# Moving the first fills of the output projection to a later scan step, and spacing them closer

## The chip, the cores and the metric

The kernel runs on one core of a Trainium2 chip. The metric is the device time of one execution in microseconds, lower is better. The times of the kernel before are 2384.92 us (median of three runs, 2384.02 to 2391.09).

## What is computed

The reference is one layer of a latent generator, with 2048 latent tokens, 256 context tokens and a width of 1024. Cut to its skeleton:

```python
h = modulate(rms_norm(x))                                # and the same of the context
u = h @ w_in                                             # columns: pool, SSD, gated DeltaNet
lat = concat([pool_branch(u), ssd(u), gdn(u)]) @ w_out   # widths 256, 384, 384
x = x + m2 * lat
h2 = modulate(rms_norm(x))
x = x + m5 * expert_choice_ffn(h2)                       # 16 experts, each takes 256 tokens
return rms_norm(x) * g
```

SSD and gated DeltaNet ("GDN") are recurrent scans in both directions. The output projection multiplies 1024 mixed columns by `w_out`. Of these the first 256 (the pool branch) are ready before the scans begin, the next 384 come from SSD, the last 384 from GDN.

## The kernel before

The work runs in five phases. Phase A projects the inputs and convolves, phase B runs the scans, phase C does the rest of the output projection and the router, phase D chooses each expert's tokens, and phase E runs the experts. Products of 32-bit numbers are made of three matmuls on split operands (`mm3`, lines 132 to 135), so every such matmul shows up on L133, L134 and L135.

The change lies in phase B. Its body is one loop over `n` (from line 1270), which issues in each pass:

- `gdn_prep(n)` (L997): the small products of GDN's step `n`, written to `xk` and `XQ`, for 36 steps;
- the SSD tiles that `ssd_seq[n]` lists: first `ssd_b` (the backward states), then from pass 9 on `ssd_f`, whose part `ssd_out` (L877 to L934) makes one of 16 output tiles and stores it to the scratch tensor `mix_d`;
- seven pieces of the triangular inverses (`gdn_inv`, L1054), which come in 7 batches, each with 31 column steps on VectorE (L1071, L1073), then transposes (L1079 to L1082) and merges;
- from pass 9 on one step of the recurrent chain, `gdn_chain` (L1115): a subtraction on VectorE (L1135, `gR`), matmuls to PSUM tiles `pc` and `po`, the new state `gS` (L1163). The last 16 steps also make GDN's output (`gdn_out`, L1180), which goes to the scratch tensor `go_d` (L1192);
- and, by a running count, fills.

A fill (`fill_0`, `fill`, L1213 to L1236) is the part of the output projection that needs no scan: the pool branch's 256 rows for one tile of 128 tokens and one half of the 1024 columns. There are 32 fills. Each loads 128 KB of `mix_d` (`fm`, L1219) and 256 KB of the input (`fx`, L1221), splits `fm` on ScalarE and VectorE (`fmh`, `fml`), makes 6 matmuls of 128x512 into the PSUM tile `po` or, for every second one, `pm`, adds on VectorE (L1226) and stores 256 KB (L1227). `po` and `pm` have one buffer each and are shared: `po` with the chain's output, `pm` with the inverses' merges. The first fill of a half also loads the weights (`load_wout`, L1204 to L1210).

The count that places the fills is this:

```python
        rate += FR                    # L1307, FR = 0.7
        if rate >= GRP:               # GRP = 2
            rate -= GRP
            for f in todo[:GRP]:
                f()
            todo = todo[GRP:]
        rate = min(rate, GRP)
        n += 1
    for f in todo:                    # whatever is left when the loop ends
        f()
```

The loop has 45 passes (0 to 44): the chain's step `k` is issued in pass 9 + k. So pairs of fills are issued in passes 2, 5, 8, 11, 14, 17, 20, 22, 25, 28, 31, 34, 37, 40 and 42, and one pair after the loop.

The order of issue isn't the order on the engines. The program is built with a scheduler that reorders by priority: an instruction's place in the program is its priority, and `tc.high_priority` moves the chain, the first steps' products and the inverses ahead. Once built, each engine and each queue runs its instructions strictly as they stand. SP's queue issues nearly all DMAs of this phase, and an issue that waits for its data holds up the issues behind it.

Phase C follows: for each tile `prep(t)` loads `mix_d` (`mx`, L1378), `go_d` (`go`, L1380) and the sums so far (L1383), transposes `go` on TensorE (L1390), and `project(t)` multiplies by the remaining rows of `w_out`. Of these rows' weights, those of the second columns' half that belong to SSD (`wr`, `woh`, `wol`) are loaded to where SSD's tiles were.

## Time and profile before

| what | value |
|---|---|
| runs listed | 2391.09, 2384.92, 2384.02 us |
| median | 2384.92 us |
| span of the profiled execution | 2391.4 us |
| time of the profiled execution beside its span | not listed apart; the first run listed, 2391.09 us, is nearest to the span |
| TensorE, VectorE, ScalarE, GpSimd busy | 87%, 72%, 45%, 35% of the span |
| phase B, from the first SSD state to the last chain step | about 780 to 1452 us |
| phase C, TensorE at work on it | 1461 to about 1650 us |

The span is the stretch between the first and the last instruction of the profiled execution. Busy shares are averages over phases with different limits, so the profile is read phase by phase.

### The profile page before, as it was taken

What the parts mean: (1) busy time and instruction counts of PE and PEld (TensorE: products, weight loads), DVE (VectorE), ACT (ScalarE), POOL (GpSimd) and SP (SyncE); (2) the same over time, 40 slices, a digit from 0 to 9 for tenths busy, and PEclk for the clock granted to TensorE, in tenths of its full rate; (3) what the DMA queues carried; (4) which work ended last, traced back from release to release, by engine and by line L of the source; (5) the groups of instructions that cost most, each with busy time, mean ns of one, the idle gap of its engine ahead of it and who ended that gap; (6) DMA issues with size and microseconds to landing.
All of it is one profiled execution on the core that took longest, in us unless ns stands there. A gap on an engine that the chain in (4) does not pass through costs nothing. (4 is left out here: it accounts for less than half of the span.)

```text
span 2391.4 us, 44610 instructions
## 1 busy us (share of the span) xinstructions
PE 2084.4 (87%) x16769; PEld 1797.7 (75%) x16769; DVE 1733.0 (72%) x3635; ACT 1077.5 (45%) x2136; POOL 834.8 (35%) x755
## 2 busy tenths in 40 slices
PE   5789999999988667999988797996499999988886
PEld 2778888888867556778777676884489999978775
DVE  7666776877754698998898765546656766788876
ACT  5443333443314345556654442554144444455552
POOL 1002333355331435454453442445221111133453
PEclk8899999999989778999997898998699999998998
DMA  7433234433323997999876675655268778788883
GB/s 236 123 92 97 80 116 122 135 102 94 94 66 80 233 245 188 217 217 221 191 191 165 163 179 192 209 199 182 84 193 243 218 227 229 222 268 284 293 272 141
DMA packets 418033, 424.72 MB, mean 178 GB/s; under 512 B 151987, under 2 KB 312602, under 8 KB 416794
## 3 DMA queue, kind: packets, MB, share of 16 engines
q1 hardware_dynamic: 398106, 368.33, 53.6%
q0 software_dynamic: 14816, 50.03, 8.0%
q10 hardware_dynamic: 4896, 3.51, 0.5%
q8 instruction: 133, 2.18, 0.4%
q14 instruction: 82, 0.67, 0.1%
HBM read 309.55 MB, written 112.22 MB: 176 GB/s over the span
## 5 line engine op out<-in xcount | busy, mean ns | idle before, releaser
L1641 ACT ACTIVATE wh<-wr 128x1024 fp32r<-128x1024 f32 x192 | 202.1, 1056 | 255.5 <-PE pgate L134 74.7
L133 PE MATMUL pj<-hTh,wh 128*128 128x512 f32 (+1 forms) x800 | 308.1, 385 | 5.3 <-ACT wh L192 4.4
L461 DVE SCALAR_TENSOR_TENSOR acc<-u,PV,acc 128x512 f32<-128x512 f32 (+1 forms) x320 | 281.9, 930 | 39.1 <-ACT acc L459 21.1
L135 PE MATMUL pj<-hTh,wl 128*128 128x512 f32 (+1 forms) x800 | 306.9, 384 | 3.5 <-DVE wl L193 3.5
L134 PE MATMUL pj<-hTl,wh 128*128 128x512 f32 (+1 forms) x800 | 309.0, 386 | 0.0
L1643 DVE TENSOR_TENSOR wl<-wr,wh 128x1024 fp32r<-128x1024 f32 x176 | 221.3, 1263 | 104.8 <-ACT wh L1641 101.4
L133 PEld LDWEIGHTS pj<-hTh,wh 128*128 128x128 f32 x800 | 153.7, 192 | 37.4 <-ACT wh L192 4.7
L135 PEld LDWEIGHTS pj<-hTh,wl 128*128 128x128 f32 x800 | 153.3, 192 | 34.5 <-DVE wl L193 4.2
L134 PEld LDWEIGHTS pj<-hTl,wh 128*128 128x128 f32 x800 | 153.4, 192 | 29.6 <-issue 0.7
L506 POOL TENSOR_TENSOR aw<-aw,sc 128x1024 f32<-128x1024 f32 x32 | 68.4, 2139 | 251.1 <-DMA aw<-in_ada_w_dram 233.0
L134 PE MATMUL pgate<-xel,wh 128*128 128x256 f32 x512 | 151.0, 295 | 3.0 <-DVE xel L193 3.0
L133 PE MATMUL pgate<-xeh,wh 128*128 128x256 f32 x512 | 149.3, 292 | 3.6 <-ACT xeh L192 3.5
L135 PE MATMUL pgate<-xeh,wl 128*128 128x256 f32 x512 | 150.3, 294 | 0.0
L133 PE MATMUL pup<-xeh,wh 128*128 128x256 f32 x512 | 148.6, 290 | 0.0
L135 PE MATMUL pup<-xeh,wl 128*128 128x256 f32 x512 | 146.9, 287 | 0.0
L134 PE MATMUL pup<-xel,wh 128*128 128x256 f32 x512 | 146.7, 287 | 0.0
L1740 POOL DMA_INDIRECT x_d<-ye,idx x30 | 48.9, 1631 | 206.0 <-DVE ye L1734 128.6
L1071 DVE TENSOR_TENSOR tmpb<-Wb,Vb 128x31 f32<-128x31 f32 (+15 forms) x217 | 107.7, 496 | 5.7 <-POOL Vb L1063 1.9
L1073 DVE TENSOR_TENSOR Vb<-Vb,tmpb 128x31 f32<-128x31 f32 (+15 forms) x217 | 108.7, 501 | 3.7
L133 PE MATMUL pdown<-wh,hh 128*128 128x512 f32 x256 | 104.6, 408 | 7.6 <-DVE ye L1734 3.3
L133 PEld LDWEIGHTS pgate<-xeh,wh 128*128 128x128 f32 x512 | 101.4, 198 | 5.0 <-ACT xeh L192 4.6
L134 PEld LDWEIGHTS pgate<-xel,wh 128*128 128x128 f32 x512 | 101.6, 198 | 3.2 <-DVE xel L193 3.2
(581 smaller groups left out, 5927.8 us busy)
## 6 DMA issues: line engine op xcount, KB each, us to landing
wr<-in_exp_w_gate_dram SPq DMA_DIRECT2D x64, 512.0 KB
wr<-in_exp_w_up_dram SPq DMA_DIRECT2D x64, 512.0 KB
wr<-in_exp_w_down_dram SPq DMA_DIRECT2D x64, 512.0 KB
aw<-in_ada_w_dram SPq DMA_DIRECT2D x32, 512.0 KB
kv<-kv_d SPq DMA_DIRECT2D x72, 192.0 KB
xb<-xb_d SPq DMA_DIRECT2D x35, 320.0 KB
wr<-in_w_in_dram SPq DMA_DIRECT2D x21, 512.0 KB
aw<-in_ada_w_dram SPq DMA_DIRECT2D x8, 1024.0 KB
```

The source lines that it names most:

```text
L133: TE.matmul(o, lh, rh, start=start, stop=False, **kw)
L134: TE.matmul(o, lh, rl, start=False, stop=False, **kw)
L135: TE.matmul(o, ll, rh, start=False, stop=stop, **kw)
L461: V.scalar_tensor_tensor(av, u[:, s0 - 2 + i:s0 - 2 + i + w], cw[:, i, cb:cb + 1], av, op0=OP.mult, op1=OP.add)
L506: G.tensor_tensor(w, w, sc2[:, :, 0:1].to_broadcast([P, KT, P]), op=OP.mult)
L1071: V.tensor_tensor(t, W[:, c + 1:, c:c + 1].to_broadcast([P, nr, ncl]), N[:, c:c + 1, :ncl].to_broadcast([P, nr, ncl]), op=OP.mult)
L1073: V.tensor_tensor(N[:, c + 1:, :ncl], N[:, c + 1:, :ncl], t, op=OP.subtract)
L1641: S.activation(wh, w, AF.Copy)
L1643: (G if nw[0] <= 16 else V).tensor_tensor(wl, w, wh.bitcast(F32), op=OP.subtract)
L1740: G.indirect_dma_start(out=x2_d, out_offset=rows_of(e, h), in_=ys[h], in_offset=None, compute_op=OP.bypass if late else OP.add)
```

## The change

The running count starts at the ninth pass (`n` = 8), and it grows by 0.85 a pass instead of 0.7. Nothing else that reaches the engines is edited; the same diff also deletes comments and docstrings, and every line below the new constant stands one line lower.

```diff
@@ -51,7 +51,8 @@
 NPS = 3
 HPP = 2000
 LATE = 7
-FR = 0.7
+FR = 0.85
+NF0 = 8
 HPI = 500
 NHI = 2
 GRP = 2
@@ -1304,7 +1305,7 @@
         if n == NSTEP:
             load_1()
-        rate += FR
+        rate += FR if n >= NF0 else 0.0
         if rate >= GRP:
```

Pairs are now issued in passes 10, 12, 15, 17, 19, 22, 24, 26, 29, 31, 33, 36, 38, 40 and 43, and again one pair after the loop: as many as before, with three pairs fewer up to pass 8.

Since priorities follow the place in the program, the scheduler now lays out the whole of phase B in another order. Three places matter here.

The first is SP's queue at the start of phase B, from the first loads of SSD's tiles (`xb`) on. `kz`, `kq` and `kqg` are GDN's loads, `fx` and `fm` a fill's. Before:

```order
L843 DMA xb<-xb_d 128x640 x2
L775 DMA fsr_d<-rows 18x6x128 x4
L1204 DMA fx<-mrow_d 128x512
L1207 DMA fx<-in_w_out_dram 128x512 x2
L843 DMA xb<-xb_d 128x640
L1219 DMA fm<-mix_d 128x256
L1010 DMA kz_6202<-qk_d 64x6x64 x2
L1010 DMA kz_6203<-qk_d 64x6x64 x2
L1221 DMA fx<-in_x_dram 128x512
L1219 DMA fm<-mix_d 128x256
L1221 DMA fx<-in_x_dram 128x512
L1219 DMA fm<-mix_d 128x256
```

After:

```order
L844 DMA xb<-xb_d 128x640 x2
L776 DMA fsr_d<-rows 18x6x128 x4
L883 DMA cb<-bc_d 128x4x128
L887 DMA zt<-z_d 128x384
L964 DMA kqg<-qk_d 64x6x128
L844 DMA xb<-xb_d 128x640
L1011 DMA kz_6202<-qk_d 64x6x64 x2
L1011 DMA kz_6203<-qk_d 64x6x64 x2
L967 DMA kqg<-qk_d 64x6x64 x2
L1011 DMA kz_6202<-qk_d 64x6x64
L982 DMA eg<-gx_d 64x12x64
L1011 DMA kz_6202<-qk_d 64x6x64
```

Up to the fourth `kz` transfer the weights' loads and a `fm` load of the first fill are gone, and loads of `cb`, `zt` and `kqg` that stood further down stand here. The first fill's loads now stand some 70 rows further down.

The second place is TensorE's end of phase B. `gS` to `pc` is the chain's product of its last step (L1133 before, L1134 now), `po<-vn` the last product of a step, `ps<-fSR` the beginning of an SSD output tile and `ps<-ident,sy` its end. Before:

```order
L1169 MATMUL po<-vn_6220,XQr 64x64 x6
L1159 MATMUL pc<-vn_6220,ke 64x64 x12
L1169 MATMUL po<-vn_6220,XQr 64x64 x6
L1133 MATMUL pc<-gS_6224,kqg 64x64 x12
L1144 MATMUL po<-gS_6224,kqg 64x64 x12
L932 MATMUL ps<-ident,sy 128x128 x3
L1151 MATMUL pc<-gR,Yt_6206 64x64 x12
L1169 MATMUL po<-vn_6221,XQr 64x64 x12
```

After:

```order
L1145 MATMUL po<-gS_6224,kqg 64x64 x12
L1152 MATMUL pc<-gR,Yt_6206 64x64 x12
L136 MATMUL pm<-fh,fml 128x512
L134 MATMUL pm<-fh,fmh 128x512
L135 MATMUL pm<-fl,fmh 128x512
L136 MATMUL pm<-fh,fml 128x512
L933 MATMUL ps<-ident,sy 128x128 x3
L852 MATMUL ps<-xw,xb 128x192 x2
L892 MATMUL ps<-fSR 128x384
L893 LDWEIGHTS identb
L893 MATMUL ps<-sneg,identb 128x384
L1170 MATMUL po<-vn_6221,XQr 64x64 x12
```

Before, `ps<-ident,sy` is the end of the last SSD tile, and it stands ahead of the chain's last two products. Now it is the end of the last tile but one, and it stands behind the chain's last product but one (`pc<-gR,Yt`); the last tile only begins (`ps<-fSR`) ahead of the chain's very last product. The last tile's own end comes 20 rows further down; the eight small products of the router's bias and then phase C's first transposes follow directly behind it.

The third place is SP's queue at the same end. Before:

```order
L934 DMA mix_d<-syT 128x384
L1192 DMA go_d<-oe_14950 2x32x384 x2
L1378 DMA mx<-mix_d 128x768
L1204 DMA wr<-mrow_d 128x512
L1207 DMA wr<-in_w_out_dram 128x512 x3
L1227 DMA x_d<-fx 128x512
L1378 DMA mx<-mix_d 128x768
L1192 DMA go_d<-oe_15029 2x32x384 x2
L1380 DMA go<-go_d 128x384
```

After:

```order
L1193 DMA go_d<-oe_15029 2x32x384 x2
L1384 DMA xo<-x_d 128x512 x2
L1402 DMA mrow_15250<-mrow_d 128x1024
L1402 DMA mrow_15252<-mrow_d 128x1024
L1406 DMA g2row<-in_norm_g_dram 128x1024
L1410 DMA rw<-in_router_w_dram 128x8x16
L1412 DMA c_15259<-mcol_d 128x16
L1384 DMA xo<-x_d 128x512 x6
L935 DMA mix_d<-syT 128x384
L1379 DMA mx<-mix_d 128x768
L1381 DMA go<-go_d 128x384
L1205 DMA wr<-mrow_d 128x512
```

Before, the store of the last SSD tile (`mix_d<-syT`) stands first and the loads of `mx` and of the weights `wr` follow ahead of the last store of GDN's output (`go_d`). Now the last `go_d` store comes first, then loads that need no scan, then the last SSD tile's store, and only behind it `mx`, `go` and `wr`.

## Rows read from the trace of the kernel before

**Rows 1.** Busy time by stretch: stretch, length, engines' busy (instructions), clock, DMA share, GB/s

```profile
780.00:892.00 112.00, 73.37 (x597) 58.90 (x597) 86.84 (x174) 46.33 (x124) 47.48 (x62) 0.72 0.99 242
892.00:1340.00 448.00, 390.61 (x5607) 339.03 (x5606) 401.14 (x810) 253.90 (x751) 203.64 (x211) 0.92 0.82 197
1340.00:1450.00 110.00, 97.95 (x1338) 86.01 (x1339) 70.82 (x151) 48.92 (x146) 53.79 (x55) 0.92 0.63 162
1475.00:1640.00 165.00, 164.10 (x958) 135.43 (x957) 80.69 (x251) 80.96 (x204) 69.37 (x29) 0.99 0.59 205
```

**Rows 2.** DMAs of 780 to 892 us: total, then issues with KB of each

```profile
DMA packets 41665, 27.13 MB, mean 242 GB/s; under 512 B 26296, under 2 KB 36712, under 8 KB 41655
...
fx<-in_x_dram SPq DMA_DIRECT2D x8, 256.0 KB
...
x_d<-fx SPq DMA_DIRECT2D x6, 256.0 KB
...
fm<-mix_d SPq DMA_DIRECT2D x9, 128.0 KB
```

**Rows 3.** Groups of DVE instructions of 780 to 892 us: count | busy, mean ns | idle before

```profile
L193 DVE TENSOR_TENSOR fml<-fm,fmh 128x256 fp32r<-128x256 f32 x8 | 4.5, 565 | 4.4 <-ACT fmh L192 4.4
...
L1226 DVE TENSOR_TENSOR fx<-po,fx 128x512 f32<-128x512 f32 x4 | 2.7, 681 | 0.6 <-PE po L135 0.6
```

**Rows 4.** The same of 1340 to 1450 us, two operations of an SSD tile

```profile
L899 DVE TENSOR_TENSOR sE<-ps,sE 128x384 f32<-128x384 f32 x8 | 4.1, 549 | 0.1
L894 DVE TENSOR_TENSOR sE<-sE,sEb 128x768 f32<-128x768 f32 x4 | 3.8, 956 | 6.1 <-ACT sEb L893 6.1
```

**Rows 5.** DVE in order of time: start, us; first inverse, first chain subtraction

```profile
813.37 2.04 DVE L1065 STREAM_TRANSPOSE Wb<-Db 64x1024 f32<-64x1024 f32 x1 [1.36 <-ACT Db L1043]
...
891.79 0.54 DVE L1135 TENSOR_TENSOR gR<-kv,pc 128x384 f32<-128x384 f32 x1
```

**Rows 6.** Who waited for whom, 892 to 1460 us: total us, times, longest

```profile
PE po L1144 <- DVE fx L1226: 12.3, 7, 3.3
...
PEld po L1144 <- DVE fx L1226: 7.6, 5, 2.6
```

**Rows 7.** PE in order of time, last SSD tile to the first output projection

```profile
1432.20 0.44 PE L891 MATMUL ps<-fSR 128*128 128x384 f32 x1
...
1449.79 0.55 PE L932 MATMUL ps<-ident,sy 128*128 128x128 f32 x3
...
1460.88 0.80 PE L133 MATMUL po<-kq,mh 128*128 128x512 f32 x1 [4.87 <-ACT mh L192]
...
1468.60 0.39 PE L134 MATMUL po<-kq,mh 128*128 128x512 f32 x1
1468.83 0.39 PE L135 MATMUL po<-kq,ml 128*128 128x512 f32 x1
1472.41 0.90 PE L1390 MATMUL ptr<-ident,go 128*128 128x128 f32 x3 [3.19 <-DMA go<-go_d]
1474.51 0.80 PE L133 MATMUL po<-Db,mh 128*128 128x512 f32 x1 [1.20 <-ACT mh L192]
```

**Rows 8.** DVE in order of time, same stretch

```profile
1440.10 0.55 DVE L921 TENSOR_TENSOR syi<-ps,syi 128x384 f32<-128x384 f32 x1
...
1448.48 0.52 DVE L928 TENSOR_SCALAR sy<-sy,sry 128x384 f32<-128x384 f32 x1
...
1449.38 0.54 DVE L1135 TENSOR_TENSOR gR<-kv,pc 128x384 f32<-128x384 f32 x1
```

**Rows 9.** SP's queue in order of time, same stretch

```profile
1450.89 0.32 SPq L934 DMA_DIRECT2D mix_d<-syT  x1
...
1453.52 0.39 SPq L1378 DMA_DIRECT2D mx<-mix_d  x1
...
1463.12 1.04 SPq L1192 DMA_DIRECT2D go_d<-oe  x2
1470.00 0.33 SPq L1380 DMA_DIRECT2D go<-go_d  x1
```

## The prediction

> **What bounds the kernel now.** The change lies in phase B, so I read the busy time by stretch first. In the head of phase B, up to the chain's first subtraction, the DMA engines are the fullest resource: share 0.99 at 242 GB/s, VectorE 86.84 of 112 us, TensorE 73.37 [rows 1]. From there to the last inverse, VectorE is busy 401 of 448 us and TensorE 391 [rows 1]: two engines near their limit, and the chain's steps wait in line with everything else. In the last 110 us the inverses are gone, VectorE falls to 71, and TensorE leads with 98 [rows 1]. Phase C then runs TensorE 164 of 165 us [rows 1], so whatever delays its start delays the end one for one. Next come the fills' own rows [rows 2, 3], the waits that fills cause [rows 6], and, instruction by instruction, the seam between phase B and phase C [rows 7 to 9].
>
> **What moves.** Nothing is added or removed: 32 fills with 6 matmuls each, the same loads and stores. Against the order before, 5 of the 6 fills that ended ahead of the chain's first subtraction now end behind it, and the SSD tiles slip back by one to two chain steps from the middle on. So I compute three terms: A, how much earlier the chain's last subtraction comes; B, what fills newly cost the chain; C, how much later phase C starts after that subtraction.
>
> **A, the chain.** In the head, the rows hold 8 `x` loads, 6 stores and 9 `fm` loads for fills [rows 2]. Up to the fourth pair of `kv` loads the new SP order has 5, 5 and 5 fewer. That is 10 x 0.262 + 5 x 0.131 = 3.3 MB, at the 242 GB/s of the stretch [rows 2] 13.5 us of DMA time. On VectorE, 6 `fml` and 5 `fx` fewer, at 565 and 681 ns [rows 3], are 3.4 + 3.4 = 6.8 us. VectorE starts the first inverse at 813.37, after an idle gap, and reaches the first subtraction at 891.79 [rows 5]; between them it is nearly always at work, so its 6.8 us are the better guide to the first subtraction than the DMA's 13.5.
>
> The fills come back later, into the stretch where VectorE is 90% busy, so the head's gain alone would be given back. What keeps it is that other work leaves: ahead of the last subtraction, the new VectorE order has two fill adds fewer (2 x 0.68 us), and of one SSD tile the addition of the exponentials (0.96), two products (2 x 0.55) [rows 4], one sum (0.55) and two scalings (2 x 0.52) [rows 8]: 5.0 us. The smaller operations of the same tile, some 20 of them, bring it to about 8 by my estimate. TensorE and GpSimd lose as much. I take **A = -8**, nearest to VectorE's rows. Its ends: -13.5 if the head is bound by its DMAs and keeps all of it, 0 if neither binds or new collisions eat it.
>
> **B, the shared bank.** The chain's products into `po` waited for a fill's add 12.3 + 7.6 us in 12 waits [rows 6], 1.66 us each. Before, 24 of the 32 fills end after the fourth chain step, from which on the chain uses `po`; now 28 do. Every second fill takes `po`, so two more meet the chain: 2 x 1.66 = 3.3 us if every wait lies on the path, 0 if none does. TensorE was the fuller engine only part of the time, so I take half, **B = +1.7**.
>
> **C, the seam.** Before, the last SSD tile began at 1432.20 [rows 7] and its store was issued at 1450.89 [rows 9], 1.5 us after the last subtraction at 1449.38 [rows 8]. SP went on to load `mx` at 1453.52 [rows 9], so TensorE did 27 matmuls of phase C from 1460.88 on, ahead of the transposes at 1472.41 and the steady stream from 1474.51 [rows 7]. At the spacing of 0.23 us (1468.60 to 1468.83 [rows 7]) these are 6.2 us of finished work, so phase C started as if at 1468.3: **18.9 us** after the last subtraction.
>
> In the new order `mx`, `go` and the weights `wr` stand on SP behind the store of the last SSD tile, and that tile begins only when the last but one has left TensorE. From the subtraction on:
> - the rest of the last tile but one. Its sum (L921) stands in the new order just ahead of the subtraction; before, 9.7 us passed from that sum to the transposes (1440.10 to 1449.79 [rows 7, 8]), with chain work in between. 4 to 8 us, taken 5.5;
> - the last tile, 1432.20 to 1450.89 before, 18.7 us with a chain step beside it [rows 7, 9]; now with little beside it. 14 to 18.7, taken 16 (the low end is an estimate: half of the 9.7 us above was waiting);
> - SP's issue of `mx` and `go`, 0.4 + 0.3 us [rows 9]; then the landing. `go` took 1470.00 to 1472.41, 2.4 us [rows 7, 9]; `mx` took 6.8 (1453.52 to the split just before 1460.88) behind other loads. 2.4 to 6.8, taken 3.4;
> - from the transposes to the stream, 2.1 us (1472.41 to 1474.51 [rows 7]).
>
> Sum 27.7, ends 23.2 and 36.3, and no matmul of phase C is done by then. **C = 27.7 - 18.9 = +8.8**, ends +4.3 and +17.4. The last store of `go_d`, issued at 1463.12 before and waited for until 1470.00 [rows 9], costs nothing now: it is issued some 10 us before `go` is asked for. The weights of the second half land behind `go`, hidden by the first half's 18 matmuls of tile 0; if they don't, 1 to 3 us more.
>
> **Sum.** -8 + 1.7 + 8.8 = **+2.5 us**. Against the profiled span of 2391.4 us that is 2393.9. The median of the runs, 2384.92, lies 0.3% below that span; I carry the difference over to the median: **2387.4 us**. About 0.3%, 7.2 us, is what a measurement of this kernel can tell from no change, so the likeliest outcome is "same": what the head wins is paid back at the seam.
>
> **Rivals.**
> 1. *The head's gain is larger and is kept.* If the DMA queue binds the head, A is -12 to -13.5, and if the last SSD tile runs at the low end, C is +4.3: -13.5 + 0 + 4.3 = -9.2, 2375.7. For it: DMA share 0.99 [rows 1]. Against it: VectorE's inverse, not the DMAs, fills the second half of the head [rows 5].
> 2. *The SSD tail decides (slower).* One mechanism: SP issues in order, and the last tile's store stands ahead of all loads that phase C needs. If the last two tiles take as long as before though the chain is over (they wait for each other through ScalarE and GpSimd, not through the chain), C is +14 to +17.4. With A = -5 and B = +3.3 this gives +12.3 to +15.7, about 2399. It decides as soon as that store is issued later than 28 us after the last subtraction. For it: the order of SP and TensorE at the seam, which is certain. Against it: 9.7 us for the end of a tile was measured with a chain step on the same engines.
> 3. *The clock (slower).* In the head the granted clock is 0.72 of full speed [rows 1], a mix of the levels 1.2 and 2.4 GHz, and the first fills are some of TensorE's work there. If their absence left the head at the lower level, the 73.37 us of TensorE less the fills' part would grow by 0.72/0.5, to over 90 of about 104 us, and TensorE would bind in places: A falls to about 0, the sum to +10.5, 2395. The Trainium skill ("TensorE: Matmul & The Clock Gate", on the HAM clock gate) says that the slow clock is the default and that sustained work lifts it, which speaks against taking work from a stretch where TensorE is often idle. Against it, in rows: the stretch is bound by loads, and fewer of them bring the prep's own matmuls closer together.
> 4. *The change does nothing, because the scheduler hides the move.* Excluded by the order: the fills do move.
>
> **How the numbers follow.** Likeliest case, within 0.3%: 0.46. Faster (rival 1, and A at -10 or better with C as taken): 0.26. Slower: 0.28, of which rival 2 has 0.21 and rival 3 0.07. The ends of A, B and C together reach from -9.2 to +20.7, but all ends at one side at once are unlikely; new collisions in the reordered 448 us stretch, which no row prices, can add a few us to either side. I take 2372 to 2403. The likeliest case's own range is 2378 to 2392.
>
> **What would show it.** In the changed kernel's profile: the first subtraction (`gR`) 6 to 12 us earlier than 891.79, and no `fx` add before it but one; the last subtraction about 8 us earlier than 1449.38 (A); waits of `po` for `fx` of about 23 us in total (B); the store of the last SSD tile (`mix_d<-syT`) as SP's last issue before `mx`, about 21 us behind the last subtraction, TensorE nearly idle in between, and the steady stream of phase C 28 us behind it (C). Phase C's own 165 us and all behind it should be unchanged. I am wrong if the last subtraction isn't earlier at all, if the store comes within 15 or beyond 28 us of it, or if phases D and E change by more than 2 us.

## The result, and the profile after

The changed kernel takes **2429.26 us** (median; its runs lie at 2426.18 to 2430.28, but for one disturbed run) beside 2386.23 of the kernel before on the same chip. The medians lie 43.0 us apart; the ratio of the runs is 1.0157, 95% interval 1.0127 to 1.0186, or some 37 us: slower, and outside the range that was given. The profiled spans, 2391.4 and 2428.5, differ by 37.1 us, and those are taken apart here. The profiled execution of the kernel before took longer than its median: if a run takes 1.8 us more than its span, as in the changed kernel (2430.28 and 2428.5), it took some 2393 us by this estimate, 7 us above the median. So the parts below can understate the loss by some us. Lines of `kernel.py` are one higher than before from line 55 on.

The landmarks, read from both traces: R1 to R35 are the chain's subtractions (`gR`), "seam" is the time from R35 to the first transposes of `go`, "C" from there to the last addition into `xo`, "experts" from the first one-hot to the last scatter of a half expert.

| | before | after | difference |
|---|---|---|---|
| R1 | 891.8 | 885.2 | -6.6 |
| end of the last inverse's column steps | 1334.7 | 1329.7 | -5.0 |
| R27 | 1331.4 | 1333.0 | +1.6 |
| R35 | 1449.4 | 1459.6 | +10.2 |
| seam | 23.0 | 36.4 | +13.4 |
| C | 171.1 | 173.5 | +2.4 |
| experts | 657.6 | 669.0 | +11.4 |

The last three and R35 add up to 37.4; what is left (-0.3) lies between and behind them. So the head won what was forecast for it, the chain lost it and 10 us more, the seam and the experts lost the rest.

Busy time by stretch in the changed kernel, columns as in [rows 1]:

```profile
780.00:892.00 112.00, 75.59 (x682) 60.51 (x683) 84.56 (x171) 48.04 (x131) 48.23 (x63) 0.75 0.91 221
892.00:1340.00 448.00, 380.48 (x5468) 331.48 (x5464) 402.38 (x791) 245.62 (x716) 197.12 (x203) 0.92 0.80 195
1340.00:1450.00 110.00, 87.90 (x1203) 77.13 (x1201) 64.99 (x140) 47.48 (x143) 49.80 (x51) 0.88 0.61 166
1475.00:1640.00 165.00, 149.12 (x840) 123.46 (x840) 78.33 (x239) 73.79 (x184) 64.34 (x94) 0.93 0.60 204
```

No engine is busier than before in any of these stretches by more than 3 us. In 1340 to 1450 TensorE does 88 us of work where it did 98, VectorE 65 where it did 71 [rows 1]: the same work comes later. From 780 us to R35, in the same columns, before and after:

```profile
780.00:1449.38 669.38, 561.32 (x7534) 483.39 (x7535) 558.19 (x1132) 349.14 (x1020) 304.91 (x328) 0.89 0.82 199
```

```profile
780.00:1459.59 679.59, 553.55 (x7465) 477.83 (x7465) 558.13 (x1110) 345.14 (x1000) 299.01 (x322) 0.89 0.78 194
```

The stretch is 10.2 us longer, though VectorE is busy as long as before and TensorE 7.8 us less, at the same granted clock (0.89): the difference is time in which the engines wait. The chain's first and last subtraction, VectorE in order of time, to set beside [rows 5, 8]:

```profile
885.20 0.55 DVE L1136 TENSOR_TENSOR gR<-kv,pc 128x384 f32<-128x384 f32 x1
...
1459.59 0.56 DVE L1136 TENSOR_TENSOR gR<-kv,pc 128x384 f32<-128x384 f32 x1 [0.34 <-PE pc L1134]
```

**The chain's end.** Between R27 and R35 8.6 us are lost. The step R30 to R31 shows how. It takes 28.9 us (11.4 before); the steps on either side of it are 6.8 and 6.7 us shorter, so that the three together lose 4.0. All engines in order of time, 1385 to 1402.5 us of the changed kernel:

```profile
1385.38 1.12 SPq L1193 DMA_DIRECT2D go_d<-oe  x2
...
1394.55 0.32 SPq L1183 DMA_DIRECT2D oe<-oe_d  x1
1394.96 1.34 SPq L982 DMA_DIRECT2D eg<-gx_d  x2
...
1400.33 0.84 ACT L984 ACTIVATE eg<-eg 128x768 f32<-128x768 f32 x1 [16.12 <-DMA eg<-gx_d]
1401.08 0.51 ACT L1186 ACTIVATE osq<-oe 128x384 f32<-128x384 f32 x1
1401.61 0.67 ACT L1096 ACTIVATE Qt<-pm 32x192 f32<-32x192 f32 x2
1401.62 0.55 DVE L1188 TENSOR_REDUCE oss<-osq 128x6 f32<-128x384 f32 x1 [13.14 <-ACT osq L1186]
...
1402.32 0.56 DVE L1136 TENSOR_TENSOR gR<-kv,pc 128x384 f32<-128x384 f32 x1
...
1402.33 0.26 PE L1099 MATMUL pm<-Yd,Qt 64*32 64x32 f32 x1 [11.62 <-ACT Qt L1096]
```

Four queues, each in its own order, stand behind one another. SyncE holds the load of `oe` (two buffers) for 6.6 us until a store of `go_d` has landed, and the gate load `eg` stands behind it. ScalarE stands at the exponential of `eg` for 16.12 us, with the output's squares `osq` and the merge's copy `Qt` behind it. VectorE stands at the sum of `osq` for 13.14 us, with R31 behind it, whose operand from TensorE was ready by 1389.5: this wait sets R31. TensorE stands at the merge for 11.62 us, with the chain's next product behind it. In the kernel before, the same instructions stand in another order:

```profile
1384.98 1.12 SPq L1192 DMA_DIRECT2D go_d<-oe  x2
...
1386.90 2.62 SPq L981 DMA_DIRECT2D eg<-gx_d  x2
...
1389.87 0.52 ACT L1185 ACTIVATE osq<-oe 128x384 f32<-128x384 f32 x1
...
1390.42 0.55 DVE L1187 TENSOR_REDUCE oss<-osq 128x6 f32<-128x384 f32 x1 [0.65 <-ACT osq L1185]
...
1393.86 0.32 SPq L1182 DMA_DIRECT2D oe<-oe_d  x1
...
1395.33 0.84 ACT L983 ACTIVATE eg<-eg 128x768 f32<-128x768 f32 x1 [3.36 <-DMA eg<-gx_d]
```

SyncE waits there too (4.2 us), but `eg` is issued ahead of the wait and not behind it, and `osq` stands ahead of `eg` on ScalarE: VectorE loses 0.65 us and ScalarE 3.36. From R27 to R35 SyncE waits as long for stores of `go_d` in both kernels:

```profile
SPq L1182 <- DMA go_d<-oe: 44.5, 9, 6.7
```

```profile
SPq L1183 <- DMA go_d<-oe: 43.1, 10, 6.6
```

The first line is the kernel before, the second the change (us, times, longest). What differs in the step above is which loads stand behind such a wait. The step R32 to R33 (26.5 us, 17.9 before) is a second case. A load of `w_out`'s rows, `gPQ`, is issued behind a 5.1 us wait of `oe`, and VectorE stands for it with the chain's new state `gS` behind, whose operand was ready by 1428.8:

```profile
1431.31 0.75 DVE L1209 SCALAR_TENSOR_TENSOR gPQ<-gPQ,wscale,gPQ 128x512 f32<-128x512 f32 x1 [5.87 <-DMA gPQ<-in_w_out_dram]
...
1434.45 1.13 DVE L1164 TENSOR_TENSOR gS<-gSG,pc 64x384 f32<-64x384 f32 x2
```

In the kernel before, the `gPQ` loads are issued ahead of that store of `go_d`, and VectorE waits 0.90 us for them. Nothing in the diff names `eg`, `oe` or `gPQ`: the scheduler has laid out the rest of the program anew behind the first moved fill.

**The seam.** SyncE's queue of the changed kernel, from the last `go_d` store on, beside [rows 9]:

```profile
1477.32 1.04 SPq L1193 DMA_DIRECT2D go_d<-oe  x2
1478.41 0.91 SPq L1384 DMA_DIRECT2D xo<-x_d  x2
1479.43 0.83 SPq L1402 DMA_DIRECT2D mrow<-mrow_d  x2
1480.31 0.43 SPq L1406 DMA_DIRECT2D g2row<-in_norm_g_dram  x1
1480.79 0.49 SPq L1410 DMA_DIRECT2D rw<-in_router_w_dram  x1
1482.18 3.29 SPq L1412 DMA_DIRECT2D c<-mcol_d  x1
1485.57 4.32 SPq L1384 DMA_DIRECT2D xo<-x_d  x6
1489.99 0.38 SPq L935 DMA_DIRECT2D mix_d<-syT  x1
1490.46 0.38 SPq L1379 DMA_DIRECT2D mx<-mix_d  x1
1490.93 0.44 SPq L1381 DMA_DIRECT2D go<-go_d  x1
```

and TensorE at the start of phase C, beside [rows 7]:

```profile
1495.96 0.90 PE L1391 MATMUL ptr<-ident,go 128*128 128x128 f32 x3 [2.17 <-DMA go<-go_d]
1496.51 0.78 PE L134 MATMUL po<-kq,mh 128*128 128x512 f32 x1
1497.08 0.63 PE L135 MATMUL po<-kq,mh 128*128 128x512 f32 x1
1497.51 0.63 PE L136 MATMUL po<-kq,ml 128*128 128x512 f32 x1
```

Three pieces make the 36.4 us. From R35 to the last store of `go_d`: 17.7 us, 13.7 before [rows 8, 9]; three fills and two SSD tiles lie among the last outputs now, one fill before. From that store to the load of `go`: 13.6, 6.9 before [rows 9], since 13 loads, the last SSD tile's store and `mx` stand ahead of it. That tile (`syT`) was ready at 1484.4, but its store stands behind six loads of `xo` and was issued at 1489.99. From that load to the transposes: 5.0, 2.4 before [rows 7, 9]. The matmuls that follow are 0.43 us apart: TensorE was busy for 5.08 of the 19 us up to 1494, and its granted clock is 0.50, 1.2 GHz, from 1496 to 1501.7. The kernel before shows 0.50 there too (1472 to 1478), so this is no part of the difference.

**The experts.** They start 26.0 us later. From the first scatter on the distance is some 28.5 us, until the row norms of the late experts mix with the weights; at the last scatter it is 37.4. Who waited for whom, 2270 to 2350 us of the changed kernel (us, times, longest):

```profile
DVE wl L1644 <- ACT wh L1642: 20.4, 6, 8.0
ACT fsq L1678 <- DMA xn<-x_d,idx: 16.0, 3, 8.3
POOL xn L1688 <- ACT xn L1687: 13.1, 4, 8.9
```

The same stretch of the kernel before, 2244 to 2324 us:

```profile
ACT fsq L1677 <- DMA xn<-x_d,idx: 16.9, 3, 6.2
DVE wl L1643 <- ACT wh L1641: 7.8, 8, 2.1
POOL xn L1687 <- ACT xn L1686: 3.5, 1, 3.5
```

ScalarE waits as long for gathered rows (`fsq`, the sum of squares), but in the new order a weight's conversion `wh` stands behind that wait, and VectorE waits 20.4 us for `wh` where it waited 7.8.

### The profile page after: what moved, and what is told of

Its sections match the earlier page's. It is cut to its first block, busy times and chain, and to the rows that moved or that the text cites. A ratio compares the mean times of both kernels' runs of the same rounds, so it can differ in the third digit from the quotient of the medians.

```text
span 2428.5 us, 44580 instructions
## 1 busy us (share of the span) xinstructions
PE 2090.4 (86%) x16769; PEld 1805.5 (74%) x16769; DVE 1743.8 (72%) x3635; ACT 1079.4 (44%) x2136; POOL 832.8 (34%) x755
## 5 line engine op out<-in xcount | busy, mean ns | idle before, releaser
L134 PEld LDWEIGHTS pj<-hTh,wh 128*128 128x128 f32 x800 | 153.2, 192 | 37.4 <-ACT wh L193 4.8
L1741 POOL DMA_INDIRECT x_d<-ye,idx x30 | 50.1, 1669 | 222.1 <-DVE ye L1735 128.6
L1072 DVE TENSOR_TENSOR tmpb<-Wb,Vb 128x31 f32<-128x31 f32 (+15 forms) x217 | 116.2, 536 | 4.5 <-POOL Vb L1064 0.6
L1074 DVE TENSOR_TENSOR Vb<-Vb,tmpb 128x31 f32<-128x31 f32 (+15 forms) x217 | 113.9, 525 | 4.1
```

Of the source, the lines that this page charges most:

```text
L134: TE.matmul(o, lh, rh, start=start, stop=False, **kw)
L1072: V.tensor_tensor(t, W[:, c + 1:, c:c + 1].to_broadcast([P, nr, ncl]), N[:, c:c + 1, :ncl].to_broadcast([P, nr, ncl]), op=OP.mult)
L1074: V.tensor_tensor(N[:, c + 1:, :ncl], N[:, c + 1:, :ncl], t, op=OP.subtract)
L1741: G.indirect_dma_start(out=x2_d, out_offset=rows_of(e, h), in_=ys[h], in_offset=None, compute_op=OP.bypass if late else OP.add)
```

## The experiments

Eighteen kernels, each timed beside the kernel before on the same chip. The expectations name theories. Theory 1: what stands behind R35 is paid at the seam. 2: fills crowded into the scan slow it. 3, later O: any new order of the program costs. W: a fill's work inside the scan is paid in full. S, S2: transfers held on SyncE lengthen the scan. Q, B: SyncE's queue or the memory queues set the seam. E: ScalarE's order sets the late experts. They count the experts from their first scatter, where the change loses 8.9 us and not the table's 11.4.

All in one table; the parts are of one profiled execution each, in us. How far they repeat is seen in `before_late4`, whose instructions up to the experts stand in the order of the kernel before, and in `after_late4`, `after_rq` and `after_go1`, which up to R35 have that of the change: R1 to R35 differs by up to 4.6 us among kernels with one order, R1 by up to 3.2 and the seam by up to 1.7.

| kernel | median | ratio to before, 95% interval | R1 | R1-R27 | R27-R35 | seam | C | experts |
|---|---|---|---|---|---|---|---|---|
| before | | | 891.8 | 439.6 | 118.0 | 23.0 | 171.1 | 657.6 |
| after | 2429.3 | 1.0127 to 1.0186 | 885.2 | 447.8 | 126.6 | 36.4 | 173.5 | 669.0 |
| start_only | 2438.5 | 1.0189 to 1.0235 | 882.5 | 455.1 | 136.7 | 39.9 | 173.0 | 667.1 |
| rate_only | 2412.5 | 1.0092 to 1.0126 | 897.0 | 451.5 | 122.5 | 22.8 | 176.9 | 654.9 |
| nf7 | 2414.4 | 1.0096 to 1.0143 | 887.4 | 452.4 | 131.1 | 26.3 | 171.2 | 657.2 |
| shift1 | 2411.8 | 1.0070 to 1.0140 | 887.4 | 455.1 | 124.8 | 27.2 | 170.8 | 655.4 |
| fr0 | 2460.2 | 1.0269 to 1.0356 | 885.1 | 435.3 | 106.7 | 115.9 | 172.5 | 657.4 |
| ssd_hp | 2402.9 | 1.0051 to 1.0088 | 889.7 | 442.0 | 128.1 | 25.4 | 171.8 | 655.6 |
| before_hp | 2392.9 | 1.0004 to 1.0032 | 896.0 | 440.9 | 117.0 | 23.0 | 172.9 | 654.2 |
| after_oe3 | 2415.7 | 1.0103 to 1.0185 | 885.9 | 450.1 | 122.8 | 36.0 | 173.1 | 654.9 |
| before_oe3 | 2409.1 | 1.0072 to 1.0135 | 891.0 | 449.2 | 122.0 | 24.2 | 176.3 | 655.0 |
| after_hp_oe3 | 2411.4 | 1.0064 to 1.0127 | 886.8 | 446.8 | 137.5 | 27.1 | 170.4 | 650.5 |
| after_gst | 2408.2 | 1.0045 to 1.0096 | 884.2 | 455.1 | 118.0 | 28.5 | 170.8 | 663.1 |
| before_gst | 2428.3 | 1.0137 to 1.0184 | 887.5 | 444.5 | 135.8 | 43.4 | 172.7 | 653.4 |
| after_got | 2415.1 | 1.0083 to 1.0134 | 887.0 | 448.7 | 109.4 | 38.6 | 172.5 | 664.1 |
| after_rq | 2430.0 | 1.0153 to 1.0207 | 883.5 | 448.4 | 128.9 | 38.7 | 172.1 | 665.6 |
| after_go1 | 2409.2 | 1.0067 to 1.0137 | 885.6 | 448.7 | 126.0 | 30.6 | 175.0 | 651.2 |
| after_late4 | 2435.0 | 1.0156 to 1.0218 | 882.4 | 450.4 | 128.6 | 38.1 | 172.6 | 668.0 |
| before_late4 | 2396.6 | 1.0018 to 1.0046 | 892.1 | 436.9 | 119.3 | 22.9 | 172.8 | 661.9 |
| before_g24_go1 | 2397.5 | 1.0017 to 1.0057 | 891.3 | 436.3 | 120.9 | 23.6 | 175.3 | 657.9 |

### The start and the rate apart, and two neighbours

`start_only` keeps the rate of before, `rate_only` the start of before; `nf7` moves the change, and `shift1` the kernel before, by one pass:

```diff
-FR = 0.85
+FR = 0.7
```

```diff
-NF0 = 8
+NF0 = 0
```

The first is `start_only`, the second `rate_only`; `nf7` has `NF0 = 7` with the rate 0.85, and `shift1` has `NF0 = 1` with 0.7.

> The start at pass 8 alone, with the rate of before (0.7). On VectorE the last SSD tile and seven fills then stand behind the scan's last subtraction R35 (in the kernel before: no SSD tile, one fill). Theory 1 (what stands behind R35 is paid at the seam, while the chain itself gains from the empty head): first subtraction 884 to 886, R35 no later than 1449, seam from R35 to the first router transposes 40 to 55 us, total 2400 to 2425. Theory 2 (fills crowded into the scan slow the chain, the tail is free): R35 later than before, seam below 30 us. Theory 3 (any new order of the program costs, wherever the fills are): about 2429 again, with a loss also in the experts.

> The rate 0.85 alone, starting with the first pass as before. Five fills stand ahead of the first subtraction and no fill behind the last one, one SSD tile behind it. Theory 1: first subtraction at 891 +-1.5 as before, seam 20 to 32 us (the SSD tile alone), total 2380 to 2400. Theory 2 (crowding slows the chain): R35 at 1455 to 1465, total 2392 to 2405. Theory 3: about 2429.

> The change, but its fills begin one pass earlier (NF0 = 7). The density of the fills in the scan is the same; on VectorE the last SSD tile and the fills fall ahead of R35 but for one fill, as in the kernel before. Theory 1 (tail order decides): seam 20 to 27 us, total 2380 to 2400. Theory 2 (density decides): R35 near 1459 as in the changed kernel, total 2410 to 2420. Theory 3: 2420 to 2435.

> The rate of before (0.7), with the fills one pass later (NF0 = 1): the smallest edit of this kind. On VectorE four fills instead of five stand ahead of the first subtraction, three instead of one behind the last. Theory O (any new order loses the good tail of before): R35 1455 to 1475, total 2395 to 2420. Theory W (time follows the count of fills inside the scan): R1 2 us earlier, R35 within 3 us of 1449, seam up by 4 to 8 us, total 2386 to 2396.

Theory 1 holds for the seam and only there: 22.8, 26.3 and 27.2 us where no more than one SSD tile and three fills stand behind R35, 39.9 where seven fills and a tile do. But R35 is late in all four, 1467 to 1474, whether the fills are dense or thin, early or late. `start_only` has 24 fills between R1 and R35, fewer than the 28 of the change, and the longer chain (591.7 against 574.4 us): Theory 2 falls. The total of `rate_only` (2412.5) fits none of the three theories; that of `nf7` (2414.4) is the one of Theory 2, but with R35 at 1470.9 and not near 1459. `shift1`, the smallest step, loses 15.4 us between R1 and R27 and 6.8 behind.

### No fills in the scan

```diff
-FR = 0.85
+FR = 0.0
```

> No fill inside the scan: the rate is 0, so all 32 stand behind the loop. Theory W (the fills' work inside the scan is paid by the chain: 28 of them between R1 and R35 in the change): R1 to R35 falls from 574 to 510 or less. Theory O (the chain is held by latencies, transfers and order, and the fills lie in its gaps): R1 to R35 is 540 to 575. In both the fills are paid behind the scan, an estimate of 3.5 to 5 us each from the 5 us spacing of the fills' adds in the kernel before: total 2480 to 2560.

R1 to R35 takes 542.0 us with one fill still inside. Against the kernel before (557.6 with 25) that is 0.65 us a fill, against the change (574.4 with 28) it is 1.20. The order differs from both, so neither is the price of a fill alone. Behind the scan 30 more fills than before make the seam 92.9 us longer, 3.1 us each. So most of a fill's time lies in the chain's gaps, and Theory W (510 us or less) falls. Five fills more or less in front of R35 are worth 3 to 6 us by these figures, less than the spread of the neighbours.

### The SSD tiles first

A higher priority for `ssd_f`, in the changed kernel (`ssd_hp`) and in the one before (`before_hp`):

```diff
-            f(t)
+            with tc.high_priority(offset=1000) if f is ssd_f else nullcontext():
+                f(t)
```

> The changed kernel with the forward SSD tiles at a higher priority. One SSD tile and two or three fills still stand behind R35 (in the change: two tiles and four fills). Theory 1: seam between that of before (23) and of the change (36), total 2405 to 2425. If the SSD tiles are late only because the scheduler ranks them low, the last y store is 20 us or more earlier than in the change (1484) and the total below 2410; if they are late because each tile waits for the one buffer of the tile before, it stays within 10 us of 1484.

> The kernel before with the SSD tiles' priority alone; its order behind R35 is that of before (no SSD tile, one fill). Seam 22 to 25. If the gain of 26 us that the priority gave the changed kernel is one of the priority, the total is 2360 to 2380; by theory O, where that was only another draw of the order, 2385 to 2415 with R35 at 1449 to 1470.

In the changed kernel the edit gives back 25.9 us of the profiled span: the seam 11.0, the experts 13.4 (which it does not touch), R1 to R35 4.3, and C 1.7, less 4.5 at the head. The last tile was ready 14 us earlier (1470.0 instead of 1484.4), between the two cases of the expectation. In the kernel before it gives nothing, so the gain was not one of the priority alone. From R28 on, `before_hp` has before's sequence of steps, fills and SSD tiles on VectorE, and its last eight steps take 117.0 us beside 118.0.

### A third buffer for the late outputs

```diff
-        oe = lt("oe2", [P, HW], 2)
+        oe = lt("oe", [P, HW], 1) if l % 3 == 2 else lt("oe2", [P, HW], 2)
```

> The changed kernel with a third buffer for the late GDN outputs (the tile of the early outputs, idle by then, takes every third step), so that SyncE waits less often for a store to land before it issues the next load. Theory S (SyncE held behind those stores is what delays the chain): the 13.3 us of go_d stores and 3.3 us of oe loads on the chain from R1 to R35 go, R35 at 1443 to 1452, total 2408 to 2420. Theory O (each order has other waits; the sum is what the scheduler's order happens to give): R35 anywhere from 1452 to 1470 with other transfers on the chain in their place, total 2415 to 2440.

> The kernel before with the same third buffer. No go_d store lies on its chain from R1 to R35. Theory S: at most the waits that follow go, total 2378 to 2388, and the order of the rest does not matter. Theory O: the order is another one from the first late step on, so that the total rises although a wait was only taken away: 2390 to 2410.

`before_oe3` is the clearest case for Theory O: a wait was only taken away, R1 to R17 is unmoved (258.6 us beside 258.8), and the new order behind it makes R35 12.8 us later and the whole 24.6 us longer by the medians. In `after_oe3` R35 and the seam are within 1 us of the change, while the experts take 14.1 us less: the experts' loss hangs on neither the chain nor the seam.

### Stores and loads on another queue

`after_gst` and `before_gst` issue each fill's store from GpSimd; `after_got` issues the output loads and stores of the last nine steps from there; `after_hp_oe3` joins the two edits above.

```diff
-        SY.dma_start(dap(dst, t * P * D + 512 * c, [[D, P], [1, 512]]), x)
+        G.dma_start(dap(dst, t * P * D + 512 * c, [[D, P], [1, 512]]), x)
```

```diff
-        SY.dma_start(oe, dap(oe_d, (31 - l) * P * HW, [[HW, P], [1, HW]]))
+        (G if l >= 23 else SY).dma_start(oe, dap(oe_d, (31 - l) * P * HW, [[HW, P], [1, HW]]))
...
-            SY.dma_start(dap(go_d, 2 * c * HW, [[HW, 2], [GW * HW, ROWS], [1, HW]]), oe[h:h + 64, :])
+            (G if l >= 23 else SY).dma_start(dap(go_d, 2 * c * HW, [[HW, 2], [GW * HW, ROWS], [1, HW]]), oe[h:h + 64, :])
```

> The changed kernel with each fill's store issued from GpSimd's queue instead of SyncE's, so that SyncE never stands still for a fill's add before the next load of the scan. Theory S2 (those held stores lengthen the scan): the 12.3 us of x_d stores leave the chain, R1 to R35 falls from 574 to 562 or less. Theory O (other waits take their place): 566 to 592. Rule of the seam (what costs is the last SSD tiles behind R35, over 30 us only with two of them or with seven fills): here no SSD tile and three fills stand behind R35, so 24 to 29 us, against 36 in the change.

> The kernel before with the same edit. Here two SSD tiles and a fill fall behind R35 in VectorE's order, as in the change and unlike in the kernel before. Rule of the seam: 31 to 40 us instead of 23, though no fill was moved by hand. Theory S2: R1 to R35 555 or less; theory O: 566 to 592, total 2400 to 2435.

> The changed kernel with both the SSD tiles' priority and the third output buffer. On VectorE no SSD tile and three fills stand behind R35: seam 24 to 29 us by the rule of the seam. The chain by theory O 565 to 590, by theory S 550 to 562. The late experts, which neither edit touches, anywhere from 6 us shorter to 9 longer than before's by theory O; 7 to 9 longer if the later start of the experts is what costs them. Total 2395 to 2415.

> The changed kernel with the loads and stores of the last nine scan steps' outputs (oe, go_d, steps R27 to R35) issued from GpSimd's queue, so that SyncE's queue no longer waits for an output before the next loads of the scan. Theory S (transfers held on SyncE make the last eight steps 126.6 us instead of 118.0): 118 or less, with under 28 us of transfers on the chain there (39.8 in the change). Theory O: 120 to 137, other waits in their place. Behind R35 stand two SSD tiles and three fills: seam 33 to 44 by the rule of the seam.

The rule of the seam held in three of the four: 28.5 and 27.1 us with no SSD tile behind R35, 38.6 with two. In `before_gst`, where no fill was moved and only the order had put two tiles there, the seam was 43.4, over the 31 to 40 expected. Theory S2 failed: R1 to R35 573.1 and 580.3 us. Theory S held in the changed order: with as many fills as in the change (7), R27 to R35 fell from 126.6 to 109.4 us. The step R30 to R31 took 18.1 us, with the outputs on GpSimd's queue and `Qt` ahead of `eg`, in order of time:

```profile
1387.16 0.61 POOL L1183 DMA_DIRECT2D oe<-oe_d  x1
1388.21 0.65 ACT L1096 ACTIVATE Qt<-pm 32x192 f32<-32x192 f32 x2
1389.67 1.30 SPq L982 DMA_DIRECT2D eg<-gx_d  x2
...
1395.05 0.84 ACT L984 ACTIVATE eg<-eg 128x768 f32<-128x768 f32 x1 [6.18 <-DMA eg<-gx_d]
```

Two things changed here together, the wait on SyncE and the place of `Qt`; their shares were not told apart. The whole of this kernel is still 1.1% above the kernel before: R1 to R27 and the seam stayed near those of the change, and the experts took 664.1 us.

### The seam: which loads, or which queue

`after_rq` issues the router's five loads from GpSimd (here one of them); `after_go1` keeps them and the `xo` loads on SyncE, behind the first `go`.

```diff
-        SY.dma_start(rw, dap(a["router_w"], 0, [[NE, P], [P * NE, KT], [1, NE]]))
+        G.dma_start(rw, dap(a["router_w"], 0, [[NE, P], [P * NE, KT], [1, NE]]))
```

```diff
-            SY.dma_start(go, dap(go_d, t * P * HW, [[HW, P], [1, HW]]))
+            G0.append(SY.dma_start(go, dap(go_d, t * P * HW, [[HW, P], [1, HW]])))
...
-            for c in range(2):
-                SY.dma_start(xt[:, 512 * c:512 * c + 512], dap(sums[c][t][1], t * P * D + 512 * c, [[D, P], [1, 512]]))
+            with tc.issue_after(G0[0].ins):
+                for c in range(2):
+                    SY.dma_start(xt[:, 512 * c:512 * c + 512], dap(sums[c][t][1], t * P * D + 512 * c, [[D, P], [1, 512]]))
...
-        SY.dma_start(rw, dap(a["router_w"], 0, [[NE, P], [P * NE, KT], [1, NE]]))
+        with tc.issue_after(G0[0].ins):
+            SY.dma_start(rw, dap(a["router_w"], 0, [[NE, P], [P * NE, KT], [1, NE]]))
```

> The changed kernel with the router's five small loads (two mrow, g2row, rw, mcol) issued from GpSimd's queue, so that on SyncE they no longer stand ahead of the first tile's mx and go. VectorE's order is that of the change up to the seam. Theory Q (6.8 us of the seam's 13.4 are SyncE's queue: the last go_d store lands at about 1484, but the first go load is issued at 1490.93, behind those loads, six xo loads and a y store): R35 stays at 1459.6, the seam falls from 36.4 to 28 to 32, total 2421 to 2426. Rival (the seam is set by the last SSD tile's y, ready at 1484.4): 35 to 37, total unchanged.

> The changed kernel with the router's loads and the xo loads held on SyncE until the first go load has been issued, as the kernel before had them; VectorE's order up to the seam is that of the change. Theory B (the first go stands in the memory queues behind some 3.7 MB of those loads, 13 loads, issued ahead of it while SyncE had nothing else: on GpSimd's queue they made its transfer 11 us instead of 5): go is issued when the last go_d store has landed, about 1484 to 1486, lands 2 to 4 us later, seam 27 to 30 us. Rival (the last SSD tile's y, 1484.4, and mx behind it decide): 32 to 36. ScalarE's order in the late experts is here that of the kernel before (no norm's sum ahead of the hh split): by theory E they lose nothing (0 to 5 us shorter than before's), total 2404 to 2414; if the later start costs them, 2418 to 2424.

Theory Q failed as put: in `after_rq` the time from the last `go_d` store to the `go` load fell from 13.6 to 9.3 us, but the load then took 11.1 us instead of 5.0, and the seam is 38.7. The Trainium skill ("DMA: Bandwidth & Descriptors", on issuing engines not being separate DMA queues) says that DMAs of every issuing engine run on the same DMA engines, and that another issuing engine saves only the time of the issue. This trace agrees for the seam, 11.1 against 5.0 us. In `after_got` the other queue came with more than that: R27 to R35 took 17.2 us less, where SyncE's loads no longer stood behind the stores' waits.

With the loads behind `go`, the seam is 30.6 us (Theory B said 27 to 30, the rival 32 to 36): 18.3 to the last store, 8.3 to the load, 4.0 to the transposes. So 5.8 us of the seam's 13.4 were loads ahead of `go`. In these 8.3 us SyncE stands 6.2 for `syT`, the last SSD tile, and issues its store, `mx` and `go` right behind: what the rival named is there too. The other 7.6 are 4.6 up to the last output's store, 1.4 from there to the load and 1.6 of transfer. Two SSD tiles are still behind R35 here. The experts took 651.2 us, 17.8 less than in the change, though they still start 22 us later than before: the late start is not their cost.

### The late norms

`after_late4` and `before_late4` split the norm's gathers from its sums and put the sums four slots later.

```diff
-                    tasks.append(lambda q=q: norm_rows(q))
+                    tasks.append(lambda q=q: NX.update({q: norm_rows(q)}))
+                    tasks += [lambda: None] * 3
+                    tasks.append(lambda q=q: norm_rest(q, NX.pop(q)))
```

> The changed kernel with the late experts' row norms split from their gathers and put four slots later; nothing ahead of the experts changes. Theory E (the late experts' 8 to 9 us are an order on ScalarE: a norm's sum waits for its gather with weight conversions queued behind it, 8.3 us at the longest): the waits of that line fall, the conversions come as in the kernel before, and the total falls by 5 to 14 us, to 2415 to 2424, with everything up to the experts unmoved. Rival (they lose because they start 28 us later, or because of memory traffic): still 7 to 9 us longer than before's, total 2427 to 2432.

> The kernel before with the same edit of the late norms as after_late4: an order of the late experts that differs from before's. Everything up to the experts is that of the kernel before. Seven other orders ended their experts 1.3 to 5.4 us sooner than before's, two 7 to 9 us later. If the edit removes what ScalarE waits for: 2378 to 2385, the only candidate to beat the kernel before; if it only draws another order: 2378 to 2395.

Both missed: 668.0 us of experts (669.0 in the change) and 661.9 (657.6 before). The wait of `wl` for `wh`, in the same stretch as above, did fall, but the experts did not gain:

```profile
DVE wl L1644 <- ACT wh L1642: 10.5, 6, 6.6
```

In `after_go1`, whose ScalarE order there is that of before, 2262 to 2342 us show:

```profile
DVE wl L1649 <- ACT wh L1647: 7.5, 8, 2.1
```

Four kernels share the change's order on ScalarE in the late experts (the change, `start_only`, `after_rq`, `after_got`), and theirs take 664.1 to 669.0 us; of the thirteen variants with other orders and no edit of the norms, twelve take 650.5 to 657.9 and `after_gst` 663.1. Theory E fits all but that one; the edit meant to remove the wait only moved the loss. The order is not the whole of it: over ScalarE's last 260 instructions `fr0`, `after_hp_oe3` and `after_go1` have that of the kernel before, and their experts take 657.4, 650.5 and 651.2 us beside its 657.6. So the experts' loss goes with the order; which wait makes it is not shown.

### Two causes removed in the kernel before

The outputs of the last eight steps on GpSimd's queue (the stores of `go_d` likewise), and the first `go` ahead of the loads as in `after_go1`:

```diff
-        SY.dma_start(oe, dap(oe_d, (31 - l) * P * HW, [[HW, P], [1, HW]]))
+        (G if l >= 24 else SY).dma_start(oe, dap(oe_d, (31 - l) * P * HW, [[HW, P], [1, HW]]))
```

> The kernel before with the outputs of the last eight scan steps on GpSimd's queue (in the changed kernel that took the steps R27 to R35 from 126.6 to 109.4 us) and the first go ahead of the router's loads. One SSD tile and one fill stand behind R35. By theories S, B and E: R27 to R35 110 to 117, seam 22 to 28, late experts 0 to 5 us shorter, total 2368 to 2385. By theory O the order loses elsewhere what it gains: 2385 to 2405.

2397.5 us: the last eight steps took 120.9 us, not 110 to 117. In the kernel before SyncE waited 44.5 us for stores of `go_d` between R27 and R35. Moving the issues to another queue gained nothing, so by this run these waits lay beside its chain. No kernel of this study beats the kernel before.

## Why the prediction was wrong

**The head** was right in size: R1 came 6.6 us earlier (6 to 12 were forecast), with one fill ahead of it. That VectorE's share of the fills is what it won was not tested: R1 came 4.4 us earlier in `nf7` with two fills ahead of it, and 4.3 in `before_gst` with all six.

**A, the chain (-8), is the step that failed.** R35 came 10.2 us later. The prediction let the head's gain stand because two fills and one SSD tile leave the chain's stretch, and priced them by VectorE's rows, as if the chain followed VectorE's work. The instructions did leave: VectorE runs 22 fewer between 780 us and R35. But it was busy as long (558.1 and 558.2 us), and the stretch grew by 10.2 us of waiting. `after_got`, with all the change's fills, shows that this time was not the fills': R1 to R35 fell from 574.4 to 558.1 us when outputs moved to another queue. What set the steps that were read (R30 to R31, R32 to R33) is which load stands behind which wait. The fills' move has drawn that anew: R1 to R35 takes 556 to 558 us in the kernel before and in `before_hp`, `before_late4`, `before_g24_go1` and `after_got`, and 570 to 592 in the change and all other variants but `fr0`. (`before_late4` has the order of the kernel before there, and `before_g24_go1` has it nearly up to R27.) "New collisions can add a few us" was in the text, with too small a number: in these kernels R1 to R35 is 12 to 34 us longer than before.

**B, the shared bank (+1.7),** had the wrong sign, though it was small. Waits of `po` for a fill's add, 892 to 1460 us:

```profile
PEld po L1145 <- DVE fx L1227: 7.7, 5, 3.1
...
PE po L1145 <- DVE fx L1227: 6.6, 5, 2.7
```

14.3 us, where 19.9 stood before [rows 6] and about 23 were forecast.

**C, the seam (+8.8),** was right in sign and inside its ends (+4.3 to +17.4): in its terms, from R35 to the end of phase C, it measured 13.4 + 2.4 = +15.8, nearest to rival 2. The last SSD store did come late (30.4 us behind R35; 21 forecast), with `mx` and `go` behind it. Two sentences were wrong. "The last store of `go_d` costs nothing": it was issued 4.0 us later behind R35, and SyncE's loads follow it on the path. And only the SSD store was seen ahead of `mx`; the 13 loads that the scheduler had put into the waiting time, 5.8 us by `after_go1`, were read past. With these gone the rest is the prediction's own mechanism, `go` behind the last tile's store.

**"Phase C's own 165 us and all behind it should be unchanged"** failed behind phase C: the experts lost 11.4 us, and four kernels with the change's order on ScalarE share that loss.

**The rivals.** Rival 2 had the right place and the right side, but with A at -5 it gave only 2399. Rival 3 fell: the head's clock is 0.75, not lower than 0.72 [rows 1]. Chances of 0.28 for slower came from adding terms of moved work; the spread of the order itself had no term.

**Open.** Which waits cost the 8.2 us between R1 and R27, where the change is 16.7 us behind the kernel before at R17 and 1.6 at R27; what the order costs in the late experts, and why those of `after_gst` and `after_late4` are long.

## What to carry to other kernels

When a scheduler lays out the program, a moved instruction reorders all that follows, also what it doesn't touch: here 18 variants lay 0.2 to 3.1% above the kernel before, also those that only took a wait away or moved fills by one pass. That none lies below it says that its order is a good one among these; it doesn't say that every new order must cost. Before pricing the moved work, read the new order of each in-order queue for loads that now stand behind a wait (a store that must land, an activation of a late load), first of all at seams and in latency-bound tails. Judge such a change by several neighbours of it, or pin the order where it matters, as the load of `go` ahead of the prefetches here.

## What the runs showed of the hardware that was not expected

A load's own time at the seam went with what was in flight. From its issue to the transposes `go` (192 KB) took 2.4 us in the kernel before, where SyncE had issued no other load for 12 us, 5.0 behind 13 loads on its own queue, and 11.1 with five of these on another queue, though it was issued 4.3 us sooner after the last output's store. And one wait passed through four engines: a wait of 6.6 us for a store on SyncE held a load, this 16.12 us of ScalarE, and this 13.14 us of VectorE and 11.62 of TensorE, none of which shows as a busy engine.
